# A hybrid attention and convolution block on one core: the second output projection takes its convolution features first, attention's splits are freed of later sums, nine background steps come sooner, and sixteen stores leave SP's queue for GpSimd's

## The chip, the cores and the metric

One core of a Trainium2 chip. The metric is the device time of one launch in microseconds. Before the change it is 2047.19 us, the median of three runs (2042.27 to 2048.67). The profiler's own execution of the same kernel took 2047.66 us, of which the span, first instruction to last, is 2045.9 us.

## The reference

One decoder layer over x of 2048 positions by 1024 features, all float32, with two mixers that read the same projection:

```python
h = rmsnorm(x, norm1_g)
q, k, v, g, a, c_b, c_c, c_h = split(h @ w_in)
o = gla_chunked(q, k, v, log_sigmoid(a @ w_gate_up + b_gate) / 16)   # 4 heads, a state carried along
o_gla = rmsnorm(o, gla_norm_g) * silu(g)                             # 512 features
o_conv = c_b * causal_depthwise_conv(c_c * c_h, conv_w)              # 512 features
x = x + concatenate([o_gla, o_conv]) @ w_out                         # the output projection
h2 = rmsnorm(x, norm2_g)
x = x + (silu(h2 @ w_gate) * (h2 @ w_up)) @ w_down
return rmsnorm(x, norm_f_g)
```

The linear attention (GLA) can be cut into chunks along the positions; a chunk needs the state that the chunk before it left. The convolution's features of a position do not depend on that state.

## The kernel before, in words

Positions lie in two halves of 1024, each of two blocks of 512. Features lie on the 128 partitions, and a product is built of 128x512 matmuls. Each float32 operand is split into a high and a low part, and three matmuls (high by high, high by low, low by high) make one product. Most of the large products are further made of seven block products in place of eight; their matmuls are L496, L497 and L498 in `product_step`.

The program runs: input projection of half 0, then of half 1; the output projection of half 0 (`first_out_proj`, L1335); that of half 1 (`out_proj`, L1411); and the feed-forward part of both halves. Between the matmuls of these, other work runs in the background. The generator `gla_half` takes the attention of one half in eight chunks of 128 positions. Each chunk fetches its data (`gla_fetch`), scales it (L1161 to L1164), makes scores (L1174, and a masked copy on VectorE at L1177), transposes (L1180, L1183), makes outputs (L1199, L1206) and the state (L1214, L1224, L1225), normalises (L1234 to L1240), and ends in `gla_finish`: transposes `ot` (L1249), the gate (L1250), a split into high and low part (L199), and two stores, of `g` and `osb`, into `s_gla` in HBM (in the profile sgla; each store takes one block and chunk).

`tick()` is called at set places of the main products and takes one background step at every second call. A generator that is wrapped in `hastened(steps, n)` (it stands in the kernel, and nothing calls it before the change) gets a step at every call whose count leaves 3 by 4 as well, until n of its steps are done. The final order on each engine is made by the tile scheduler from a model of the times; `behind(marks)` keeps an instruction behind those in `marks`. `gla_finish` puts its split behind `last_out + last_plus`, the newest sum of the main product at the time the program is written down.

`first_out_proj` takes the weights in four steps of d0 = 0, 2, 4, 6 (two output blocks of 128 features each). In each it makes seven products of the convolution features (four ticks), then 48 matmuls of the heads (L1386, L1392). `plus` (L1355) adds each result onto the residual `y` on VectorE; the finished `y` is stored as x1 (L1400; sx in the profile), and its squares are summed (`sum_squares`, L1269 to L1273).

`out_proj` has no seven products: for each of eight blocks k of 128 features it takes 12 matmuls in each d0 (L1421, L1422, L1424). Blocks 0 to 3 are the heads, from sgla, and 4 to 7 the convolution features, from sm. `build_mix` issues the sixteen loads (`op`, 512 KB each) in the order of k. During it the background normalises the x1 of half 0 for the feed-forward part (`h2_first`: `column_rstd` with the matmuls L218, the loads `h<-sx`, and L939 on VectorE).

Loads and stores all go through `load` (L152) and `store` (L155) on SP's queue, which issues them in order. Each waits for what it needs, and all that stands behind it on SP waits too; a DMA of SP also waits for the one that was issued eight before it. GpSimd (POOL) issues no DMA before the change.

Of the kernel before, what the change touches and what calls it, by code (L numbers as in the profile page):

```python
# [25 lines left out]
KD = D // P  # L26
# [4 lines left out]
GROUPS = (0, 2, 5, 8)  # L31
LAST_GROUP = GROUPS[-1]
EARLY = 7
EPS = 1e-6


# [17 lines left out]
def tile_hymba_block(ctx, tc, x, xt, win, wa, wgu, wout, wffn, wdown, wdown_first, small, out):  # L54
# [1022 lines left out]
    def in_proj(half, ops, raw=None, between=(), rest=None):  # L1077
        def units():
            if half == 0:
                yield unit(win[2], ops, raw=raw, between=between, rest=rest)  # L1080
            for u in range(0 if half else 3, 12):
                yield unit(win[u], ops, after=2 if half and u < 3 else None)

        units = units()
        for dst, i0 in ((s_kq, 0), (s_kq, 2), (s_v, 0), (s_v, 2)):
            if half == 0 and dst is s_kq:
                continue
            for r, j, c, p in next(units):
                store(dst[2 * half + j][i0 + r][:], settled(c, p)[:])
        for i0 in (0, 2):  # L1090
            for r, j, c, p in next(units):
                store(s_g[2 * half + j][i0 + r][:], silu(c, p)[:])
        if half:
            background.append(gla_half(half))
        for i0 in (0, 2):
            cc = {(r, j): settled(c, p) for r, j, c, p in next(units)}
            ch = {(r, j): c for r, j, c, _ in next(units)}
            for r in range(2):
                i = i0 + r
                left = halo[:, i, :]  # L1100
                for j in range(2):
                    s = tp.tile([P, PB + 2], F32, name="u", tag="t")
                    dve.tensor_tensor(s[:, 2:], ch[r, j][:], cc[r, j][:], ALU.mult)
                    act.activation(s[:, 0:2], left, AF.Copy)
                    left = s[:, PB : PB + 2]
                    y = cc[r, j]
                    act.activation(y[:], s[:, 0:PB], AF.Copy, scale=col(C_CW + i))
                    for n in (1, 2):
                        dve.scalar_tensor_tensor(
                            y[:], s[:, n : n + PB], col(C_CW + 4 * n + i), y[:], ALU.mult, ALU.add  # L1110
                        )
                if half == 0:
                    act.activation(halo[:, i, :], left, AF.Copy)
            for r, j, c, _ in next(units):
                y = cc[r, j]
                dve.tensor_tensor(y[:], c[:], y[:], ALU.mult)
                dst = s_mix[2 * half + j][i0 + r]
                if half:
                    pair_out(y, dst)
                else:  # L1120
                    store(dst[:], y[:])
# [136 lines left out]
    def plain_weights(src, n):  # L1258

        raw = rawp.tile([P, 4, PB], F32, name="raw", tag="raw")  # L1260
        load(raw[:, 0:n, :], src)
        for i in range(n):
            h = weight_quarter(raw[:, i, :])
            for k in range(4):
                yield h[:, 0, k * P : (k + 1) * P], h[:, 1, k * P : (k + 1) * P]
# [69 lines left out]
    def first_out_proj(y, conv, heads):  # L1335

        ssq = [
            tiny.tile([P, PB], F32, name=f"ssx{j}", tag=f"ssx{j}", bufs=1) for j in range(2)
        ]
        for d0 in range(0, KD, 2):  # L1340
            raw = raw_weights(wout[d0 // 2]).rearrange("p a (b e c) -> p (a b) e c", e=2, c=P)
            quads = [raw[:, k : k + 2, e, :] for e, k in ((0, 4), (0, 6), (1, 6), (1, 4))]
            w = unit_weights(None, quads)
            wh = [weight_quarter(raw[:, 0:HEADS, e, :]) for e in range(2)]

            def mul(i, o=None):
                first = o is None
                o = bank() if first else o
                n, m = PRODUCTS[i]
                for k in range(2):  # L1350
                    product_step(o, w[n], conv[m], k, first)
                return o

            def plus(at, o):
                last_plus[:] = [dve.tensor_tensor(y[at][:], o[:], y[at][:], ALU.add)]  # L1355
                last_out[:] = last_plus
                all_plus.extend(last_plus)

            oa = mul(0)
            plus((0, 0), oa)  # L1360
            ob = mul(1)
            plus((1, 1), ob)
            due("T3")
            tick()
            mul(2, oa)
            plus((0, 1), oa)
            due("B22")
            o = mul(3)
            tick()
            mul(4, oa)  # L1370
            plus((1, 1), oa)
            due("T4")
            mul(5, ob)
            plus((0, 1), ob)
            tick()
            mul(6, oa)
            plus((1, 0), oa)
            tick()
            following = residual(d0 + 2) if d0 + 2 < KD else None
            for e in range(2):  # L1380
                po = [bank() if e or j else o for j in range(2)]
                for k in range(HEADS):
                    c = slice(k * P, (k + 1) * P)
                    for j in range(2):
                        for part in range(2):
                            pe.matmul(  # L1386
                                po[j][:], wh[e][:, 0, c], heads[k][j][:, part, :],
                                start=k + part == 0 and e + j > 0, stop=False,
                                skip_group_check=True,
                            )  # L1390
                    for j in range(2):
                        pe.matmul(  # L1392
                            po[j][:], wh[e][:, 1, c], heads[k][j][:, 0, :], start=False,
                            stop=k == HEADS - 1, skip_group_check=True,
                        )
                    if k % 2:
                        tick()
                for j in range(2):
                    plus((e, j), po[j])
                    store(s_x1[j][d0 + e][:], y[e, j][:])  # L1400
                    sum_squares(ssq[j], y[e, j][:], d0 + e == 0)
            y = following
        return ssq

    def build_mix():
        def pair(b, k):
            return load_pair(s_gla[b][:, k] if k < HEADS else s_mix[b][k - HEADS])

        return [[pair(2 + j, k) for j in range(2)] for k in range(KD)]

    def out_proj(ops, ahead, rest):  # L1411
        ssq, half = [], 1
        ws = chain.from_iterable(plain_weights(wout[u], 4) for u in range(4))
        for d0 in range(0, KD, 2):
            o = {(e, j): bank() for e in range(2) for j in range(2)}
            for k in range(KD):
                for e in range(2):
                    wh, wl = next(ws)
                    for j in range(2):
                        m = ops[k][j]  # L1420
                        pe.matmul(o[e, j][:], wh, m[:, 0, :], start=k == 0, stop=False)  # L1421
                        pe.matmul(o[e, j][:], wh, m[:, 1, :], start=False, stop=False)  # L1422
                    for j in range(2):
                        pe.matmul(  # L1424
                            o[e, j][:], wl, ops[k][j][:, 0, :], start=False, stop=k == KD - 1
                        )
                if k == 3:
                    ys = {}
                    for e in range(2):
                        for j in range(2):  # L1430
                            ys[e, j] = tt("y")
                            load(ys[e, j][:], xt[2 * half + j, :, d0 + e, :])
                for _ in range(1 if d0 == KD - 2 else 2):
                    next(rest if d0 == KD - 2 else ahead, None)
                tick()
            if d0 == 0:
                ssq += [
                    tiny.tile([P, PB], F32, name=f"ssx{j}", tag=f"ssx{j}", bufs=1)
                    for j in range(2)
                ]  # L1440
            for e in range(2):
                for j in range(2):
                    b, dt = 2 * half + j, d0 + e
                    y = ys[e, j]
                    dve.tensor_tensor(y[:], y[:], o[e, j][:], ALU.add)
                    store(s_x1[b][dt][:], y[:])
                    sum_squares(ssq[j], y[:], dt == 0)
        return ssq
# [506 lines left out]
```

## Time and profile before

| | before |
|---|---|
| three runs, median (lowest to highest) | 2047.19 us (2042.27 to 2048.67) |
| profiled execution: time / span | 2047.66 / 2045.9 us |
| PE / PEld / DVE / ACT / POOL busy | 99 / 81 / 76 / 48 / 1 % of the span |
| mean granted clock of TensorE | 0.995 |
| second output projection begins on PE | 665.57 us |

The page gives busy shares for each engine and groups of instructions by source line. The views used here beside it are the list of waits of one engine (who it waited for, microseconds in total, how many times, the longest), the timeline (start, duration, instruction, and in square brackets the idle time ahead of it with what ended it), and tables of windows (a stretch in microseconds from the start of the span, its length, busy time of PE, PEld, DVE, ACT and POOL with their instructions, the granted clock as a share, the share of the DMA engines that was busy, GB/s). Matmuls overlap in the pipeline: one of 128x512 has a row of 0.39 us, but the next begins 0.23 us after it.

### The profile page before, as it was taken

What the parts mean: (1) busy time and instruction counts of PE and PEld (TensorE: products, weight loads), DVE (VectorE), ACT (ScalarE), POOL (GpSimd) and SP (SyncE); (2) the same over time, 40 slices, a digit from 0 to 9 for tenths busy, and PEclk for the clock granted to TensorE, in tenths of its full rate; (3) what the DMA queues carried; (4) which work ended last, traced back from release to release, by engine and by line L of the source; (5) the groups of instructions that cost most, each with busy time, mean ns of one, the idle gap of its engine ahead of it and who ended that gap; (6) DMA issues with size and microseconds to landing.
All of it is one profiled execution on the core that took longest, in us unless ns stands there. A gap on an engine that the chain in (4) does not pass through costs nothing.

```text
span 2045.9 us, 27026 instructions
## 1 busy us (share of the span) xinstructions
PE 2021.6 (99%) x9275; PEld 1658.7 (81%) x9275; DVE 1563.3 (76%) x2837; ACT 973.5 (48%) x1941; POOL 10.3 (1%) x17
## 2 busy tenths in 40 slices
PE   9999999999999999999999999999999999999998
PEld 8788878787877788888888888887888888888886
DVE  7888877668867597778777688887777777778886
ACT  6664455755534244444444453334444444454345
POOL 0000000000000000000000000000000000000001
PEclk9999999999999999999999999999999999999999
DMA  7356886644684893445445576577454444486653
GB/s 262 122 201 220 283 302 190 196 134 157 229 296 160 323 326 140 170 169 207 171 168 195 184 294 240 189 279 294 150 180 170 153 151 170 166 334 226 247 216 129
DMA packets 194634, 429.35 MB, mean 210 GB/s; under 512 B 20448, under 2 KB 67776, under 8 KB 185024
## 3 DMA queue, kind: packets, MB, share of 16 engines
q1 hardware_dynamic: 193776, 426.97, 58.9%
q8 instruction: 73, 1.20, 0.2%
q10 hardware_dynamic: 720, 0.66, 0.1%
q14 instruction: 65, 0.53, 0.1%
HBM read 279.69 MB, written 147.85 MB: 209 GB/s over the span
## 4 chain that ended last, share of the span: by engine, by line
PE 89%; DMA 5%; DVE 3%; ACT 2%; issue 1%; SPq 1%; POOL 0%; POOLq 0%; DVEq 0%; ACTq 0%
PE mm L496 26%; PE mm L498 26%; PE mm L497 26%; PE mm L1421 1%; PE mm L1424 1%; PE mm L1422 1%; DMA raw<-in_win_dram 1%; DMA op<-shT 1%; PE a_ps L1020 1%; PE mm L801 1%; PE mm L803 1%; PE mm L802 1%; PE mm L1741 1%; PE mm L1386 1%; PE o_ps L1199 1%
## 5 line engine op out<-in xcount | busy, mean ns | idle before, releaser
L496 PE MATMUL mm<-op,wq 128*128 128x512 f32 x2499 | 974.3, 393 | 4.1 <-ACT wq L198 1.5
L497 PE MATMUL mm<-op,wq 128*128 128x512 f32 x2499 | 972.3, 390 | 0.6 <-DVE op L199 0.5
L498 PE MATMUL mm<-op,wq 128*128 128x512 f32 x2499 | 962.1, 390 | 0.3
L198 ACT ACTIVATE wq<-raw 128x512 fp32r<-128x512 f32 (+2 forms) x628 | 361.8, 581 | 599.5 <-PE mm L498 477.6
L496 PEld LDWEIGHTS mm<-op,wq 128*128 128x128 f32 x2499 | 469.5, 188 | 107.6 <-ACT wq L198 4.6
L498 PEld LDWEIGHTS mm<-op,wq 128*128 128x128 f32 x2499 | 469.5, 188 | 99.9 <-DVE wq L199 1.9
L497 PEld LDWEIGHTS mm<-op,wq 128*128 128x128 f32 x2499 | 469.8, 188 | 98.6 <-DVE op L199 2.6
L199 DVE TENSOR_TENSOR wq<-raw,wq 128x512 fp32r<-128x512 f32 (+2 forms) x628 | 389.8, 625 | 165.2 <-ACT wq L198 163.6
L530 DVE TENSOR_TENSOR c<-mm,c 128x512 f32<-128x512 f32 x196 | 134.6, 687 | 71.8 <-PE mm L498 67.1
L530 DVE TENSOR_TENSOR y<-mm,y 128x512 f32<-128x512 f32 x185 | 126.5, 687 | 54.1 <-PE mm L498 53.8
L542 ACT ACTIVATE c<-mm 128x512 f32<-128x512 f32 x198 | 115.5, 589 | 33.1 <-PE mm L498 30.6
L448 DVE TENSOR_TENSOR raw<-raw 128x512 f32<-128x512 f32 (+2 forms) x190 | 116.5, 619 | 2.1
L198 ACT ACTIVATE wq<-s 128x512 fp32r<-128x512 f32 (+2 forms) x100 | 58.0, 580 | 101.3 <-PE mm L498 91.5
L448 DVE TENSOR_TENSOR s<-raw 128x512 f32<-128x512 f32 (+2 forms) x95 | 58.9, 620 | 33.9 <-DMA raw<-in_wffn_dram 17.8
L199 DVE TENSOR_TENSOR op<-op 128x512 fp32r<-128x512 f32 x100 | 66.3, 683 | 3.7 <-ACT op L198 3.5
L199 DVE TENSOR_TENSOR wq<-s,wq 128x512 fp32r<-128x512 f32 (+2 forms) x100 | 62.4, 624 | 2.2 <-ACT wq L198 1.4
L198 ACT ACTIVATE op<-op 128x512 fp32r<-128x512 f32 x100 | 59.2, 622 | 9.1 <-DMA op<-siT 3.2
L448 DVE TENSOR_TENSOR raw<-s,raw 128x512 f32<-128x512 f32 (+2 forms) x95 | 59.0, 621 | 1.3
L597 ACT ACTIVATE sg<-mm 128x512 f32<-128x512 f32 x26 | 15.5, 597 | 85.1 <-PE mm L498 85.1
L597 ACT ACTIVATE c<-c 128x512 f32<-128x512 f32 x78 | 48.9, 629 | 13.3 <-DVE c L530 10.6
L1421 PE MATMUL mm<-op,wq 128*128 128x512 f32 x128 | 50.8, 399 | 4.5 <-DMA op<-sgla 4.5
L1422 PE MATMUL mm<-op,wq 128*128 128x512 f32 x128 | 50.5, 395 | 0.0
(240 smaller groups left out, 1689.2 us busy)
## 6 DMA issues: line engine op xcount, KB each, us to landing
raw<-in_wffn_dram SPq DMA_DIRECT2D x44, 1024.0 KB, 5.9
sa_B<-so SPq DMA_DIRECT2D x47, 512.0 KB, 3.7
op<-sa_B SPq DMA_DIRECT2D x47, 512.0 KB, 6.9
raw<-in_win_dram SPq DMA_DIRECT2D x22, 1024.0 KB, 6.0
sa_T<-so SPq DMA_DIRECT2D x44, 512.0 KB, 4.4
op<-sa_T SPq DMA_DIRECT2D x44, 512.0 KB, 6.7
raw<-in_wdown_dram SPq DMA_DIRECT2D x24, 768.0 KB, 5.5
sx<-y SPq DMA_DIRECT2D x48, 256.0 KB, 4.1
```

The lines of the kernel that those rows point to most:

```text
L198: last_hi[:] = [act.activation(hi, src, AF.Copy)]
L199: last_lo[:] = [dve.tensor_tensor(lo, src, hi.bitcast(F32), ALU.subtract)]
L448: dve.tensor_tensor(*args)
L496: pe.matmul(o[:], wh, xh, start=first and k == 0, stop=False, skip_group_check=True)
L497: pe.matmul(o[:], wh, xl, start=False, stop=False, skip_group_check=True)
L498: return pe.matmul(o[:], wl, xh, start=False, stop=k == n - 1, skip_group_check=True)
L530: last_plus[:] = [dve.tensor_tensor(t[:], o[:], t[:], ALU.add)]
L542: last_out[:] = [act.activation(t[:], o[:], AF.Copy)]
L597: last_silu[:] = [act.activation(s[:], c[:], AF.Silu)]
L801: pe.matmul(acc[:], wq[:, 0, c], p[:, 0, :], start=first, stop=False)
L1421: pe.matmul(o[e, j][:], wh, m[:, 0, :], start=k == 0, stop=False)
L1422: pe.matmul(o[e, j][:], wh, m[:, 1, :], start=False, stop=False)
```

## The change

There are four edits. Line numbers are those of before; after the change they stand one to two higher.

1. **Features.** `LATE_HEADS` orders the blocks of `out_proj` as 4, 5, 6, 7, 0, 1, 2, 3. `build_mix` loads in that order, the matmuls follow it, `plain_weights` takes its quarters of the weights as 2, 3, 0, 1, and the marks for first and last go by the place in the order.
2. **Pace.** The attention of half 1 goes into the background as `hastened(gla_half(1), 9)`.
3. **Splits.** In `first_out_proj` only the sums of d0 = 0 are noted in `last_plus` and `last_out`; those of later d0 are not, so `gla_finish`'s split is no longer put behind them.
4. **Stores.** The sixteen stores of x1 in `first_out_proj` are issued by `pool.dma_start`.

```diff
+LATE_HEADS = 4, 5, 6, 7, 0, 1, 2, 3
...
-            background.append(gla_half(half))
+            background.append(hastened(gla_half(half), 9))
...
-        for i in range(n):
+        for i in (n // 2 + i if i < n // 2 else i - n // 2 for i in range(n)):
             h = weight_quarter(raw[:, i, :])
...
-                last_plus[:] = [dve.tensor_tensor(y[at][:], o[:], y[at][:], ALU.add)]
-                last_out[:] = last_plus
-                all_plus.extend(last_plus)
+                summed = dve.tensor_tensor(y[at][:], o[:], y[at][:], ALU.add)
+                all_plus.append(summed)
+                if d0 == 0:
+                    last_plus[:] = last_out[:] = [summed]
...
-                    store(s_x1[j][d0 + e][:], y[e, j][:])
+                    pool.dma_start(s_x1[j][d0 + e][:], y[e, j][:])
...
-        return [[pair(2 + j, k) for j in range(2)] for k in range(KD)]
+        return {k: [pair(2 + j, k) for j in range(2)] for k in LATE_HEADS}
...
-            for k in range(KD):
+            for n, k in enumerate(LATE_HEADS):
...
-                        pe.matmul(o[e, j][:], wh, m[:, 0, :], start=k == 0, stop=False)
+                        pe.matmul(o[e, j][:], wh, m[:, 0, :], start=n == 0, stop=False)
...
-                            o[e, j][:], wl, ops[k][j][:, 0, :], start=False, stop=k == KD - 1
+                            o[e, j][:], wl, ops[k][j][:, 0, :], start=False, stop=n == KD - 1
...
-                if k == 3:
+                if n == 3:
```

The instructions are the same in number and kind on PE, VectorE and ScalarE, and stand in another order only between the middle of the second input projection and the start of the feed-forward part. SP loses 16 DMAs, and POOL gains them.

The first place is SP's queue at the end of `first_out_proj`. Rows show the line, the destination and source with their buffer numbers, and the shape: `sgla3` is the attention's output of the last block of 512 positions, `op` an operand of `out_proj`, `sx` an x1 tile, `y` its source. Before the change:

```order
L155 DMA sx0_6_175<-y_6536 128x512
L155 DMA sx1_6_183<-y_6540 128x512
L155 DMA sgla3_234<-gt_6448 512x1x128
L155 DMA sgla3_234<-osb_6730 512x1x128
L152 DMA op_6837<-sgla3_234 128x1024
L152 DMA op_6839<-sgla2_233 128x1024
L152 DMA op_6841<-sgla3_234 128x1024
```

The same place after the change:

```order
L156 DMA sgla3_234<-gt_6308 512x1x128
L156 DMA sgla3_234<-osb_6590 512x1x128
L153 DMA op_6847<-sm2_3_212 128x1024
L153 DMA op_6849<-sm3_3_216 128x1024
L153 DMA op_6851<-sgla2_233 128x1024
L153 DMA op_6853<-sgla3_234 128x1024
L153 DMA op_6855<-sgla2_233 128x1024
L153 DMA op_6857<-sgla3_234 128x1024
```

The stores of x1 are gone from between, and two loads of convolution features stand ahead of those of the heads.

The second place is SP's queue at the start of `first_out_proj`, where `raw` is a block of w_out and `kq` belongs to a chunk of the attention. Before the change:

```order
L155 DMA sgla2_233<-gt_5313 512x1x128
L152 DMA y_5760<-in_xt_dram 128x512
L152 DMA y_5968<-in_xt_dram 128x512
L152 DMA raw_6384<-in_wout_dram 128x2048
L152 DMA y_5970<-in_xt_dram 128x512
```

After the change:

```order
L153 DMA op_6835<-sm2_0_209 128x1024
L153 DMA op_6837<-sm3_0_213 128x1024
L153 DMA op_6839<-sm2_1_210 128x1024
L153 DMA op_6841<-sm3_1_214 128x1024
L153 DMA y_5850<-in_xt_dram 128x512
L153 DMA y_6058<-in_xt_dram 128x512
L153 DMA op_6843<-sm2_2_211 128x1024
L153 DMA y_6060<-in_xt_dram 128x512
L153 DMA raw_6474<-in_wout_dram 128x2048
```

Five of the eight loads of sm for `out_proj` stand here now, ahead of the weights of the next d0.

The third place is PE at the passage into `out_proj`. `tot` is the sum for `column_rstd`; op_6835 is before the change the first head's operand, and after it that of the first convolution block. Before:

```order
L1392 MATMUL mm_6800<-op_5800,wq_6669 128x512
L1386 MATMUL mm_6799<-op_5802,wq_6669 128x512 x2
L1386 MATMUL mm_6800<-op_5804,wq_6669 128x512 x2
L1392 MATMUL mm_6799<-op_5802,wq_6669 128x512
L1392 MATMUL mm_6800<-op_5804,wq_6669 128x512
L1421 MATMUL mm_6867<-op_6835,wq_6873 128x512
L1422 MATMUL mm_6867<-op_6835,wq_6873 128x512
L1424 MATMUL mm_6867<-op_6835,wq_6873 128x512
L1421 MATMUL mm_6868<-op_6837,wq_6873 128x512
```

After the change, where the heads begin inside `out_proj`:

```order
L1426 MATMUL mm_6869<-op_6847,wq_6900 128x512
L1426 MATMUL mm_6870<-op_6849,wq_6900 128x512
L219 MATMUL tot_6936<-ssx0_5896,ones_92 128x512
L219 MATMUL tot_6947<-ssx1_5897,ones_92 128x512
L1423 MATMUL mm_6867<-op_6851,wq_6957 128x512
L1424 MATMUL mm_6867<-op_6851,wq_6957 128x512
L1423 MATMUL mm_6868<-op_6853,wq_6957 128x512
```

The first operand from sgla (op_6851) is now needed 48 matmuls of `out_proj` after its start, where before it is needed by the first one. The last transposes `ot` of the attention (L1249; after the change L1250) stand 30 matmuls ahead of the first one of `out_proj` before the change, and 114 ahead of it after the change.

## The prediction

> **What bounds the kernel now.** I read the page first, then the list of PE's waits, then tables of windows for the granted clock, then the timelines of PE, SP and VectorE around each wait. Two lines of the page and five of the list of waits:
>
> ```profile
> span 2045.9 us, 27026 instructions
> PE 2021.6 (99%) x9275; PEld 1658.7 (81%) x9275; DVE 1563.3 (76%) x2837; ACT 973.5 (48%) x1941; POOL 10.3 (1%) x17
> ```
>
> ```profile
> PE mm L1421 <- DMA op<-sgla: 4.5, 1, 4.5
> PE o_ps L1199 <- ACT c L542: 2.1, 1, 2.1
> PE v_ps L1183 <- issue: 1.4, 1, 1.4
> PE mm L1386 <- DMA op<-sgla: 0.4, 1, 0.4
> PE mm L496 <- DVE osb L1240: 0.3, 1, 0.3
> ```
>
> The kernel is bound by PE: 2021.6 of 2045.9 us are busy, and the change takes no matmul away. It can only gain where PE stands idle, or where an idle spell has slowed PE's clock. These five waits are all that PE has in the stretch that is reordered. The windows tell what a wait costs beyond its own length:
>
> ```profile
> 488.00:495.00 7.00, 6.82 (x19) 5.48 (x20) 4.72 (x10) 1.62 (x5) 0.00 (x0) 0.52 0.40 152
> 600.00:620.00 20.00, 18.28 (x97) 14.10 (x96) 14.29 (x37) 10.59 (x33) 0.00 (x0) 1.00 0.78 259
> 668.00:671.00 3.00, 0.05 (x1) 0.05 (x1) 0.64 (x2) 0.00 (x0) 0.00 (x0) 0.63 0.88 235
> 671.00:676.00 5.00, 5.00 (x11) 3.61 (x12) 0.00 (x0) 0.00 (x0) 0.00 (x0) 0.54 1.00 382
> ```
>
> After the waits of 2.1 and 4.5 us the granted clock falls to about half for some 7 us, though PE is busy again. Across the waits of 1.4 and 0.3 us (600 to 620) it stays at 1.00. So somewhere between 1.7 and 2.1 us of idleness a second price begins. After the wait at 486 us PE loses 7.00 x 0.48 = 3.4 us by the clock. After the one at 666 us much of the slow time falls into the idleness itself, and what is lost is 5.00 x 0.46 = 2.3 us.
>
> [...]
>
> **The long wait at the start of the second output projection.** PE, then SP, then VectorE:
>
> ```profile
> 658.41 0.49 PE L1249 MATMUL ot<-ident,osb 128*128 128x128 f32 x3
> ...
> 665.57 0.39 PE L1421 MATMUL mm<-op,wq 128*128 128x512 f32 x1
> 665.80 0.39 PE L1422 MATMUL mm<-op,wq 128*128 128x512 f32 x1
> 666.03 0.39 PE L1424 MATMUL mm<-op,wq 128*128 128x512 f32 x1
> 670.95 0.80 PE L1421 MATMUL mm<-op,wq 128*128 128x512 f32 x1 [4.54 <-DMA op<-sgla]
> ```
>
> ```profile
> 663.24 0.52 SPq L155 DMA_DIRECT2D sgla<-osb  x1
> 665.85 1.28 SPq L152 DMA_DIRECT2D op<-sgla  x3
> 667.22 1.16 SPq L155 DMA_DIRECT2D sx<-y  x2
> 668.43 2.86 SPq L152 DMA_DIRECT2D op<-sgla  x4
> 672.47 8.45 SPq L152 DMA_DIRECT2D op<-sm  x8
> 682.82 4.17 SPq L152 DMA_DIRECT2D y<-in_xt_dram  x4
> 687.94 4.16 SPq L152 DMA_DIRECT2D h<-sx  x4
> ```
>
> ```profile
> 662.53 0.68 DVE L199 TENSOR_TENSOR osb<-osb,gt 128x512 fp32r<-128x512 f32 x1
> ```
>
> The chain is serial: the last chunk's transposes at 658.41, its split at 662.53, its store at 663.24, the load that waits for the store at 665.85, and the matmul at 670.95, 12.5 us in all. PE has only 30 matmuls (7.2 us) to cover it. After the change 114 matmuls stand between these transposes and the first L1421, and the first 48 of the projection need sm alone. Matmuls follow each other by 0.23 us (665.57, 665.80, 666.03), so the chain gets 162 x 0.23 = 37 us in place of 7.2. Even with two loads of sm ahead of those of sgla on SP (8.45 us for eight, so 2.1) the margin is above 20 us. **This wait goes: 4.54 + 2.3 = 6.8 us.** What is late next there? The convolution operands: five of their eight loads stand about 90 us before their use, a sixth follows soon, and the last two stand ahead of the heads' loads.
>
> **The wait at 614 us.** PE, VectorE, SP:
>
> ```profile
> 615.39 0.63 PE L1183 MATMUL v_ps<-ident,vt 128*128 128x128 f32 x4 [1.39 <-issue]
> 616.36 0.47 PE L496 MATMUL mm<-op,wq 128*128 128x512 f32 x1 [0.33 <-DVE osb L1240]
> ```
>
> ```profile
> 590.18 0.42 DVE L448 TENSOR_TENSOR s<-raw 128x256 f32<-128x256 f32 x1
> ...
> 612.88 0.42 DVE L448 TENSOR_TENSOR s<-raw 128x256 f32<-128x256 f32 x1 [4.26 <-DMA raw<-in_wout_dram]
> ...
> 616.46 0.68 DVE L1355 TENSOR_TENSOR y<-mm,y 128x512 f32<-128x512 f32 x1
> ...
> 661.92 0.69 DVE L1355 TENSOR_TENSOR y<-mm,y 128x512 f32<-128x512 f32 x1 [0.76 <-PE mm L498]
> ```
>
> ```profile
> 576.78 0.33 SPq L152 DMA_DIRECT2D raw<-in_wout_dram  x1
> ...
> 597.46 1.21 SPq L155 DMA_DIRECT2D sx<-y  x1
> ...
> 604.51 0.36 SPq L152 DMA_DIRECT2D raw<-in_wout_dram  x1
> ```
>
> VectorE stood 4.26 us on a block of w_out that SP had issued only at 604.51; the attention's state (L1224) and norm (L1240) queued behind it, and PE waited 1.39 + 0.33 = 1.7 us for banks and operands. In the changed order that L448 stands behind L1224 and L1240 of the chunk, and x1 stores no longer stand ahead of the block on SP. **I count the 1.7 us as gained**, with nothing as the other end, since a late block then holds later sums instead. The 0.4 us of L1386 I leave where it is.
>
> **The wait at 486 us stays.** It comes from VectorE, which has no idle time ahead of it:
>
> ```profile
> 485.63 0.40 PE L497 MATMUL mm<-op,wq 128*128 128x512 f32 x1
> 488.18 1.19 PE L1199 MATMUL o_ps<-vt,scores 128*128 128x128 f32 x4 [2.15 <-ACT c L542]
> ```
>
> ```profile
> 470.00:488.00 18.00, 15.95 (x76) 12.27 (x74) 18.00 (x40) 10.32 (x25) 0.00 (x0) 1.00 0.72 239
> ```
>
> VectorE is busy for 18.00 of 18 us, and the order of VectorE up to that point is unchanged; the two matmuls ahead of L1199 move behind it. That shifts at most 0.1 us between idleness and slow clock, so 2.15 + 3.4 us remain.
>
> **The added costs.** The nine sooner steps bring no instruction; the first three chunks after 488 us come some 12, 22 and 26 us earlier, by the matmuls ahead of them at 0.23 us each. Their VectorE and ScalarE work moves into this stretch:
>
> ```profile
> 540.00:560.00 20.00, 20.00 (x106) 15.78 (x107) 18.23 (x42) 13.51 (x36) 0.00 (x0) 1.00 0.97 364
> 560.00:600.00 40.00, 39.44 (x213) 30.71 (x212) 29.68 (x70) 14.39 (x46) 0.00 (x0) 1.00 0.89 295
> ```
>
> VectorE has 1.8 us left in 540 to 560 and 10.3 in 560 to 600; half a chunk more in the former is about 3 us, which spills by about 1 us into the latter. I take nothing; the cover is the freedom behind 560, and if it is gone the price is the second case.
>
> The five early loads of sm are 2.6 MB in 560 to 600, where the DMA engines already are busy 0.89 of the time at 295 GB/s. At that rate they need 8.9 us, and 0.11 x 40 = 4.4 are free; so up to 4.5 us of lateness. I take nothing, because the block asked for at 576.78 was used at 590.18, and the one that is held up by the most traffic, asked for at 604.51, was ready at 612.88, 8.4 us after: 5 us of freedom for the former, about the same 4.5. The other end is the third case.
>
> The sixteen stores on POOL have no row before. Two DMA rows of the page bound them:
>
> ```profile
> sx<-y SPq DMA_DIRECT2D x48, 256.0 KB, 4.1
> y<-in_xt_dram SPq DMA_DIRECT2D x32, 256.0 KB, 5.7
> ```
>
> Who waits for a store is the next load of the same buffer. The tightest is the sum at 616.46, whose buffer serves the sum at 661.92: 45 us, of which store and load take 4.1 + 5.7. A store could come 35 us late and hold nobody. In the other direction, SP is free of sixteen issues, of which a long one is 1.21 us (597.46); that speeds loads that nobody but the wait at 614 us waits for. So nothing, both ways.
>
> [...]
>
> In the projection itself `column_rstd` moves behind 48 matmuls, 11 us after the start; it stood at 674.96, 9.4 us after it, because of the wait. The h loads at 687.94 stood behind fifteen operand loads, six of which are now gone from there, so the work of the feed-forward's operands is not later. Nothing.
>
> **The sum.** 2047.66 - 6.8 - 1.7 = 2039.1 us on the profiled execution, which is 0.5 us above the median of the runs. I predict 2039.
>
> **The rivals.**
>
> 1. *Forecast*, 0.56: 2036 to 2041. The lower end takes the 0.4 us as well and as much of smaller waits; the upper has the wait at 614 only shifted.
> 2. *A new short wait*, 0.20. The denser chunks before 600 us make PE stand once as at 486 us. For it speaks VectorE at 18.23 of 20; against it, of PE's waits between 500 and 600 us none is for VectorE now. 2.1 + 3.4 = 5.5 us: 2044.6.
> 3. *Late weights, slower than before*, 0.18. The five sm loads push the next block of w_out back by the 4.5 us worked out above. VectorE then stands 4.26 + 4.5 = 8.8 us where it stood 4.26. Of 4.26 us PE felt 1.7, so 2.5 are slack, and it would feel 6.2 and then half clock, 3.4: 2039.1 + 9.6 = 2048.7. With both later blocks late it is 2058. It decides from a lateness of about 3.5 us on, where loss and gain are equal. For it: 0.97 and 0.89 of DMA share. Against it: the 5 us of freedom that the first of these blocks has.
> 4. *Starved stores*, 0.03. If a store on POOL took over 35 us, SP would stand at the load behind it, and PE would wait once with half clock: 2044.6 or more.
> 5. *The heads still late*, 0.03. If sgla's loads are held by the operand buffers that the last products of `first_out_proj` use, the wait only moves 48 matmuls on: 2039.1 + 6.8 = 2045.9.
>
> **How the numbers follow.** What a measurement of this kernel can tell from no change is about 0.3%, 6.1 us: 2041.1 to 2053.3. The first case lies under it: faster 0.56. The second, fourth, fifth and the third with one block (0.08 of its 0.18) lie between: 0.34. The third with two lies above: 0.10. The range from 2036 to 2049 holds all but the last of these.
>
> **What would show it.** In the changed profile, L1421's wait on op<-sgla is gone from PE's list, and the windows between 640 and 700 us show a clock of 1.00; L1199 still waits about 2 us near 486 us, with one stretch of half clock behind it, the only one there. If there is a second stretch of half clock between 500 and 640 us, the forecast is wrong by 5 us or more; whether VectorE's wait ahead of it ends on raw<-in_wout (third case) or on nothing but its own work (second) tells which. POOL's stores that land much later than 4.1 us would speak for the fourth.

## The result, and the profile after

The changed kernel takes 2040.64 us, the median of seven runs (2037.56 to 2043.84), against 2046.37 us for the kernel before (2042.27 to 2048.67, seven runs). The ratio is 0.9971 with a 95% interval of 0.9959 to 0.9983: faster by 0.29%, just short of the 0.3% that I had taken as the least that can be told, though the interval lies clear of 1. The forecast was 2039.0 in a range of 2036 to 2049. The profiled execution took 2040.49 us with a span of 2038.3, 7.6 us below the span before.

The page's first lines, and PE's list of waits after the change, without the waits at the start and the end of the program:

```profile
span 2038.3 us, 27053 instructions
PE 2016.1 (99%) x9275; PEld 1656.9 (81%) x9275; DVE 1566.9 (77%) x2837; ACT 974.4 (48%) x1941; POOL 19.1 (1%) x33
```

```profile
PE mm L1388 <- DMA op<-sgla: 3.1, 1, 3.1
PE o_ps L1200 <- ACT c L543: 3.0, 1, 3.0
...
PE sc L1175 <- DVE kq L1165: 0.5, 1, 0.5
PE mm L497 <- DVE c L531: 0.5, 1, 0.5
```

L1421's wait on sgla (4.5 us) is gone, and so are those of L1183 (1.4) and L1240 (0.3). The wait at 486 us is still there, at 3.0 us and not 2.1. And one that was 0.4 us has become 3.1: L1388, the first projection's heads, on their loads. L1175 has a new wait of 0.5 us. The windows show what the two long ones cost beyond their length, and that the stretch around the second projection is whole:

```profile
488.00:495.00 7.00, 6.47 (x26) 5.25 (x27) 5.07 (x11) 2.48 (x6) 0.00 (x0) 0.76 0.49 184
575.00:580.00 5.00, 5.00 (x19) 3.95 (x20) 0.00 (x0) 0.60 (x1) 0.00 (x0) 0.66 1.02 405
640.00:660.00 20.00, 20.00 (x90) 16.55 (x89) 13.17 (x24) 6.34 (x11) 1.38 (x3) 1.00 0.80 298
660.00:680.00 20.00, 20.00 (x87) 15.84 (x86) 9.43 (x15) 6.69 (x12) 1.86 (x4) 1.00 0.77 304
```

The third last column is the granted clock. Behind the wait at 486 us it costs 7.00 x 0.24 = 1.7 us (3.4 before), and behind the new one 5.00 x 0.34 = 1.7. From 640 to 680 us PE is busy throughout at full clock; 660 to 680 holds 87 matmuls, where it held 56 before the change:

```profile
660.00:680.00 20.00, 15.46 (x56) 11.46 (x55) 9.09 (x15) 6.52 (x10) 0.00 (x0) 0.83 0.78 264
```

After the change, the last chunk's transposes, its store, the loads and the start of the projection, from the timelines of PE and SP:

```profile
639.23 0.60 PE L1250 MATMUL ot<-ident,osb 128*128 128x128 f32 x4
...
665.54 0.39 PE L1423 MATMUL mm<-op,wq 128*128 128x512 f32 x1
```

```profile
643.56 0.51 SPq L156 DMA_DIRECT2D sgla<-osb  x1
646.01 1.01 SPq L153 DMA_DIRECT2D op<-sm  x2
647.37 3.72 SPq L153 DMA_DIRECT2D op<-sgla  x6
652.16 0.33 SPq L153 DMA_DIRECT2D raw<-in_wout_dram  x1
652.59 2.02 SPq L153 DMA_DIRECT2D op<-sgla  x2
```

The heads' loads are all issued by 654.6, 11 us before the projection and some 22 before their first use. But the projection begins at 665.54, and before it began at 665.57: nothing that was gained ahead of it is left by then. The groups of the first matmul of a block (L1421 before, L1423 after) show that nearly the whole gain lies inside the projection:

```profile
L1421 PE MATMUL mm<-op,wq x128: 389/389/795, 665.6 to 760.5; 128*128 128x512 f32 x128
```

```profile
L1423 PE MATMUL mm<-op,wq x128: 389/389/791, 665.5 to 753.4; 128*128 128x512 f32 x128
```

From its first to its last: 94.9 us before, 87.9 after, 7.0 less, of a span that is 7.6 less.

### The profile page after: what moved, and what is told of

Read it like the earlier page. It is cut to its first block, busy times and chain, and to the rows that moved or that the text cites. A ratio compares the mean times of both kernels' runs of the same rounds, so it can differ in the third digit from the quotient of the medians.

```text
span 2038.3 us, 27053 instructions
## 1 busy us (share of the span) xinstructions
PE 2016.1 (99%) x9275; PEld 1656.9 (81%) x9275; DVE 1566.9 (77%) x2837; ACT 974.4 (48%) x1941; POOL 19.1 (1%) x33
## 4 chain that ended last, share of the span: by engine, by line
PE 91%; DMA 3%; DVE 3%; ACT 2%; issue 0%; SPq 0%; POOL 0%; POOLq 0%; DVEq 0%; ACTq 0%
PE mm L497 26%; PE mm L499 26%; PE mm L498 26%; PE mm L1426 1%; PE mm L1423 1%; PE mm L1424 1%; PE mm L1388 1%; DMA op<-shT 1%; PE a_ps L1021 1%; PE mm L802 1%; PE mm L804 1%; PE mm L803 1%; DMA op<-sgla 1%; PE mm L1743 1%; DMA raw<-in_win_dram 1%; PE o_ps L1200 1%
## 5 line engine op out<-in xcount | busy, mean ns | idle before, releaser
L497 PE MATMUL mm<-op,wq 128*128 128x512 f32 x2499 | 974.4, 393 | 2.5 <-ACT c L543 1.2
L497 PEld LDWEIGHTS mm<-op,wq 128*128 128x128 f32 x2499 | 469.5, 188 | 105.1 <-ACT wq L199 3.7
L1423 PE MATMUL mm<-op,wq 128*128 128x512 f32 x128 | 50.2, 392 | 0.0
```

What stands on the lines that cost most here:

```text
L497: pe.matmul(o[:], wh, xh, start=first and k == 0, stop=False, skip_group_check=True)
L1423: pe.matmul(o[e, j][:], wh, m[:, 0, :], start=n == 0, stop=False)
```

## The experiments

Each has its own runs of the kernel before on the same chip; ratios are to these. The first four take the change apart.

**Edit 1 alone.** Against the change:

```diff
-            background.append(hastened(gla_half(half), 9))
+            background.append(gla_half(half))
...
-                    pool.dma_start(s_x1[j][d0 + e][:], y[e, j][:])
+                    store(s_x1[j][d0 + e][:], y[e, j][:])
```

and the three lines of `plus` as before the change.

> Edit 1 alone: the convolution features come first in the second output projection, the other three edits are undone. The last transposes of the attention stand 33 rows-worth of matmuls ahead of the projection, as before the change, and the heads are needed 48 matmuls into it: 81 x 0.23 = 18.6 us for a chain that took 12.5. First theory (edits 1 and 2 each take the wait at the start of the projection away alone): 6.8 us faster than before, ratio 0.9967; the waits at 614 us (1.7) and at 486 us stay, and no wait of 3 us on the heads of half 0. Rival (both are needed, since two loads of 512 KB stand ahead of the heads'): a wait on sgla remains inside the projection, and the gain is under 3.5 us, ratio above 0.9983.

Measured: ratio 0.9973 (0.9962 to 0.9984), median 2041.75 against 2047.15. The wait on sgla in the second projection is gone. Three of its waits:

```profile
PE o_ps L1200 <- ACT c L543: 2.1, 1, 2.1
PE v_ps L1184 <- DMA vt<-sv: 1.6, 1, 1.6
PE mm L1387 <- DMA op<-sgla: 1.3, 1, 1.3
```

So one edit brings about the gain of all four (0.9971), within the noise. The first theory holds for the projection. It missed that the wait of the first projection's heads grows here too, from 0.4 to 1.3 us, without the sooner steps.

**Edit 2 alone.** The heads stay first, and `plus` and the stores are as before:

```diff
-LATE_HEADS = 4, 5, 6, 7, 0, 1, 2, 3
+LATE_HEADS = 0, 1, 2, 3, 4, 5, 6, 7
```

with `plain_weights` in the old order.

> Edit 2 alone: nine background steps come sooner, the heads stay first, splits and stores as before. The last transposes stand 119 matmuls ahead of the projection, 27 us. First theory: the wait at the start of the projection goes (6.8 us) and that at 614 us (1.7), but the new wait for the heads of half 0 near 572 us comes with its half clock (3.1 + 1.8 - 0.4 = 4.5): about 4 us faster than before, ratio 0.998. Rival (the new wait comes from the early loads of sm, edit 1): no wait near 572 us, 8.5 us faster, ratio 0.9958.

Measured: 0.9973 (0.9963 to 0.9982), 2042.84 against 2047.15: 4.3 us by the medians and 5.5 by the ratio, near the first theory's 4 us, but not by its sum. Three of its waits:

```profile
PE o_ps L1200 <- ACT c L543: 3.0, 1, 3.0
...
PE mm L1387 <- DMA op<-sgla: 1.7, 1, 1.7
PE v_ps L1184 <- issue: 1.7, 1, 1.7
```

The wait of the first projection's heads is 1.7 us and not 3.1, and the windows from 560 to 600 us show a clock of 1.00; the wait of v_ps, which I took to be gone, is there with 1.7. The wait in the second projection is gone by this edit alone too: from 660 to 680 us PE is busy for 20.00 us at a clock of 1.00. Each of the two edits takes the same 6.8 us, and the second to come finds nothing left.

**Without edit 2**, and **without edit 4**. One undoes the pace, the other puts the x1 stores back on SP; each is a line of the diff above.

> The change without edit 2 (edits 1, 3 and 4 are in). First theory: the wait at the start of the projection is gone, the new wait near 572 us is not there, that at 614 us stays or goes with the stores that have left SP: 6.8 to 8.5 us faster than before, ratio 0.9958 to 0.9967, at or below the whole change's. Rival (the new wait is not edit 2's): a wait of about 3 us near 570 us, and 3 us faster than before, ratio 0.9985.

> The change without edit 4: the sixteen x1 stores stay on SP. First theory (the stores' queue is worth nothing): as the whole change within 1 us, ratio to before 0.997, the same waits on PE. Rival (edit 4 carries part of the gain, because SP is free of sixteen issues ahead of the weights of w_out): the wait for raw near 614 us is back and 1.7 us or more are lost against the whole change, ratio 0.998 or above.

Measured: without the pace 0.9967 (0.9955 to 0.9980), 2041.28; without GpSimd's stores 0.9963 (0.9951 to 0.9976), 2040.62; both against 2047.15. Neither differs from the whole change. Without the pace the heads' wait near 570 us is 0.5 us, and the time is no better. Its profile has a wait of 2.2 us for ScalarE's split of an operand near 1396 us, which the change's profile doesn't have. That lies in the feed-forward part, where PE's order is the same in both, so one profile of each can't tell whether it belongs to the edit.

Without GpSimd's stores the heads' wait is 1.1 us, so PE's waits are not the same, as the first theory had them; and the rival is half right, as the weights of w_out are late again, though no time is lost. VectorE, and the wait of PE that follows:

```profile
617.72 0.43 DVE L449 TENSOR_TENSOR s<-raw 128x256 f32<-128x256 f32 x1 [2.35 <-DMA raw<-in_wout_dram]
```

```profile
PE v_ps L1184 <- DVE raw L449: 1.3, 1, 1.3
```

The timelines of PE in that kernel and in the changed one, at the heads' wait:

```profile
570.64 0.43 PE L1181 MATMUL kt_ps<-ident,kq 128*128 128x128 f32 x2
572.22 0.73 PE L1388 MATMUL mm<-op,wq 128*128 128x512 f32 x2 [1.14 <-DMA op<-sgla]
```

```profile
571.33 0.43 PE L1181 MATMUL kt_ps<-ident,kq 128*128 128x128 f32 x2
574.85 0.99 PE L1388 MATMUL mm<-op,wq 128*128 128x512 f32 x2 [3.09 <-DMA op<-sgla]
```

And SP in the same two kernels, ahead of the load that is waited for:

```profile
563.04 1.85 SPq L153 DMA_DIRECT2D gt<-sg  x4
...
566.95 0.39 SPq L153 DMA_DIRECT2D op<-sgla  x1
```

```profile
564.44 3.14 SPq L153 DMA_DIRECT2D gt<-sg  x4
...
569.11 0.40 SPq L153 DMA_DIRECT2D op<-sgla  x1
```

PE's order is the same in both, and the loads take 5.3 and 5.7 us to the matmul. The difference is when SP comes to the load: the four loads of `gt` ahead of it took SP 1.85 us in one and 3.14 in the other. The DMA engines were full up to 560 us in both (shares of 1.02 and 1.03 from 540 to 560), but not at these loads: from 562 to 568 us their share in the change is 0.19 to 0.48. Why SP took longer there is not shown. x1 stores play no part yet: GpSimd issues its first at 593.60. So with PE's order the same the wait varies; in the six kernels with that order, or with that order and the repeated transposes below, it is 1.1 to 3.1 us.

**Edit 3 undone**, with the three lines of `plus` as before the change.

> The change without edit 3: the attention's splits stay behind the sums of all four steps. PE's order is the same as with it. First theory: no difference beyond 1 us, ratio to before 0.997, PE's waits as in the whole change. Rival (the splits were late and held stores of sgla): a wait on sgla at the start of the heads in the second projection, and 2 us or more lost.

Measured: 0.9967 (0.9956 to 0.9979), 2039.83 against 2046.77, and waits as in the whole change (3.0 there is 2.9 here, 3.1 is 2.8). Edit 3 is worth nothing here.

Four further kernels try to take away the two waits that the change left.

**The attention later.** `pause(n)` gives n empty background steps, with n = 3 and n = 4:

```diff
+            background.append(pause(3))
             background.append(hastened(gla_half(half), 9))
```

> The change, and three empty background steps ahead of the attention of half 1, so that its first chunk comes later: 82 matmuls (19 us) now stand between that chunk's transposes (v_ps) and its outputs (o_ps), where none stood. First theory (the wait at 486 us costs its idleness and the half clock behind it): both go, 3.0 + 1.8 to 3.4 us, and the chain of the last chunk has 32 + 48 matmuls, 18 us for 12.5: 5 to 6 us faster than the whole change, ratio to before 0.9945. Rival (VectorE is the bound from 460 us on, so the wait is only put off to a later chunk): another wait of 2 us or more between 500 and 620 us with half clock, and the time of the whole change, ratio 0.997.

> As with three empty steps, but four: the first chunk's scores stand 84 matmuls later, its outputs 24 matmuls (5.5 us) behind its transposes, and the last transposes 26 matmuls ahead of the second projection, 74 ahead of the first need of the heads (17 us). First theory: the wait at 486 us is gone, VectorE having 5.5 us at a time when it is not full; no wait for sgla in the projection; ratio 0.9945. Rival (17 us are too few for the chain with two loads of sm ahead of it): a wait of 2 us or more on op<-sgla inside the projection, ratio 0.997 or above.

Measured: three steps 0.9992 (0.9983 to 1.0001), four 1.0016 (1.0007 to 1.0025). The rival of the first kernel has the mechanism right and the time too short (0.997); for the second kernel both theories miss. The wait of o_ps is gone from both lists, and others stand in its place. With four, in the list of waits:

```profile
PE mm L497 <- DVE y L1357: 5.9, 1, 5.9
PE mm L497 <- DVE kvs L1226: 2.6, 1, 2.6
PE mm L497 <- ACT c L543: 2.6, 2, 1.4
PE sc L1176 <- issue: 2.4, 1, 2.4
```

Later chunks meet the weights of the first projection on VectorE, and PE waits there for sums and for the attention's state. With four steps VectorE itself stands 9.7 us, in three waits, on blocks of w_out. The place of the attention's start is worth more than the one wait at it.

**Convolution stores on GpSimd too.**

```diff
-                    pair_out(y, dst)
+                    pair_out(y, dst, pool.dma_start)
```

where `pair_out` takes the issuing function as an argument.

> The change, and the stores of the convolution features of half 1 (sm) also on GpSimd's queue; they stood between the loads of half 0's heads on SP. First theory (those loads are late by their place in SP's queue): each is issued 1 to 3 us sooner, and the wait on op<-sgla near 572 us falls from 3.1 us to under 1.5 and brings no half clock: 2 to 4 us faster than the whole change, ratio 0.9955. Rival (that wait's length is the DMA engines' load at the time, 1.03 of 540 to 560, and differs from run to run): the same time as the whole change within 1 us, ratio 0.997.

Measured: 0.9987 (0.9978 to 0.9996), 2044.38 against 2046.77, so both theories miss: it loses some of the gain. The heads' wait falls only to 2.1 us, a new one of 2.6 (L497, on VectorE's hsq) stands behind it, and the windows from 580 to 600 show 0.91 of the clock. The scheduler also placed the attention's pieces in another order, so this run doesn't tell what the queue alone does.

**PE kept busy.** In `gla_scores` of the first chunk alone, the transposes into kt_ps are repeated once its copy has been taken; nothing reads them:

```diff
+        for i in range(8 if (b, t) == (2, 0) else 0):
+            pe.transpose(kt_ps[:, i % 2, :], kq[:, i % 2, :], ident[:])
```

This was put into the change with 8 and with 16 transposes, into edit 1 alone with 8, and into the change without edit 4 with 16.

> The change, and eight transposes (about 1 us) that repeat the first chunk's kt_ps after it has been copied, while PE waits near 486 us; their result is not read. All else on PE stands in the same order. First theory (the drop of the clock follows a spell without any work on PE of some 2 us): the wait of 2.96 us is cut into pieces under 2, the clock between 488 and 495 stays at 1.00, and 1.7 to 3.4 us go: ratio to before about 0.996. Rival (the drop comes with any light load of that stretch): the clock still falls behind 488 us, ratio 0.997.

> As with eight, but sixteen repeated transposes, about 2 us. First theory: no idle piece over 1 us is left there, the clock stays at 1.00, and o_ps starts no later than before (VectorE and ScalarE set that), so 1.7 to 3.4 us go: ratio about 0.996, as with eight or better. Rival: the transposes come too late, push o_ps back by up to 1 us and save nothing: ratio 0.9975.

> Edit 1 alone, and the eight repeated transposes near 486 us. First theory: edit 1 alone takes the wait at the start of the second projection away (6.8 us, in the profile of edit 1 alone), the wait of 2.15 us at 486 us is cut and with it its half clock (1.7 to 3.4 us), and no new wait with half clock comes near 572 us: the fastest of all, 8 to 9 us faster than before, ratio 0.9958. Rival (the waits at 570 to 615 us, 1.3 to 1.6 us each, are as dear as the whole change's): ratio 0.997.

> Edits 1, 2 and 3 with the sixteen repeated transposes, and the x1 stores on SP as before the change. First theory (edit 4 is worth nothing, the repeated transposes save the half clock near 486 us): clock 1.00 between 488 and 495 us, the time of the kernel with sixteen transposes and GpSimd's stores within 1 us, ratio 0.996. Rival (GpSimd's stores carry a gain once the half clock is gone): ratio above 0.997.

| | ratio (95%) | median, before |
|---|---|---|
| the change, 8 transposes | 0.9963 (0.9949 to 0.9977) | 2038.3, 2047.49 |
| the change, 16 transposes | 0.9961 (0.9948 to 0.9974) | 2037.58, 2047.49 |
| edit 1 alone, 8 | 0.9965 (0.9952 to 0.9977) | 2039.48, 2047.49 |
| edits 1, 2, 3, with 16 | 0.9955 (0.9941 to 0.9968) | 2037.93, 2047.54 |

The order of the rest of the program is the same but for a few matmuls next to this place. PE's timeline with 8, and then the window behind it:

```profile
485.41 1.09 PE L1188 MATMUL kt_ps<-ident,kq 128*128 128x128 f32 x8 [0.96 <-ACT ee L1185]
487.41 0.68 PE L1202 MATMUL o_ps<-vt,scores 128*128 128x128 f32 x4 [0.90 <-ACT c L543]
```

```profile
488.00:495.00 7.00, 7.00 (x40) 5.65 (x40) 5.39 (x13) 3.27 (x12) 0.00 (x0) 1.00 0.33 124
```

Counted from the transposes into v_ps the attention's outputs start no sooner (3.6 us after them, 3.5 in the change), but the idle time is cut into 0.96 and 0.90 us, and the clock stays at 1.00: 40 matmuls in these 7 us, where the change had 26. It does so in all four, while all eight profiles without such transposes or empty steps have a lowered clock there (0.83 to 0.91 from 480 to 500 us). So at this place the lowered clock goes with the idle spell of 2.1 to 3.0 us: nothing else was taken away. All four medians lie 1 to 3 us under the change's; the intervals overlap with its own, so that they beat it is likely and not shown, while each beats the kernel before. Edit 1 alone with 8 was expected to be the fastest of all and has the highest median of the four; its profile has a wait of 1.9 us near 612 us, of v_ps on its load.

## Why the prediction was right, and where it was not

**What bounds the kernel**: right. PE is busy for 99% in both, and the whole difference is in its waits and their clock.

**The long wait, 6.8 us**: right, in place and size. The projection is 7.0 us shorter from its first to its last matmul, and it is edit 1 that does it, or edit 2; either is enough. I had added the room that both give (114 and 48 matmuls) without asking what each gives alone.

**The wait at 614 us, 1.7 us counted as gained, with nothing against it**: this is the step that failed. It is gone from the changed profile, but the projection starts at the same moment as before. What took its place was the wait of 0.4 us at L1386, of which I wrote that I leave it where it is: it became 3.1 us and 1.7 us of lowered clock. I looked for new waits at VectorE and at the weights, and costed the denser chunks there. I didn't follow what they do to the loads of the *first* projection's heads: those stand on SP behind the fourteen small loads of a chunk, and in PE's order one v_ps and one pair of heads fewer stand ahead of the use that waits. In the profiles without the sooner steps this wait is 0.4 to 1.3 us, in the eight with them and without empty steps 1.1 to 3.1. The second rival had such a wait at nearly the right price (2.1 + 3.4 there, 3.1 + 1.7 here) from other parts; its cause was not VectorE but a DMA.

**The wait at 486 us, unchanged at 2.15 + 3.4**: right in that it stays, and wrong in its parts, of which I let at most 0.1 us move; it measured 3.0 + 1.7.

These do not add up to the equal start: 1.7 us are gained at 614 us and 0.9 at 486 (5.5 before, 4.7 after), and 4.4 are lost at 572 (3.1 + 1.7 - 0.4) and 0.5 at the new wait of L1175, so the projection should start about 2.3 us later. It doesn't. By the starts of PE's rows from 480 us to the projection, the waits and the lowered clock taken off, the same matmuls took about 2.5 us less after the change (an estimate), some 1.1 of it in the attention's outputs (L1199 and L1206). Why they did stays open. That the time lies in the first case all the same is in part luck: a loss that the sum hadn't was made up by gains that it hadn't either.

**Late weights**: did not happen in the change. No wait on raw is in PE's list, with a DMA share of 1.03 from 540 to 560 us and 1.05 from 580 to 600. Nor did the early loads of sm make the heads late: SP issues them from 579.88 us on, behind the load that PE waits for at 572.

**GpSimd's stores, nothing**: right. They took 5.4 us to land in the median (2.5 to 7.7), against 4.1 for such stores before, and nobody waited; with them on SP the time is the same. But the stores do bear on the wait at 614 us. In the six profiles with them on SP VectorE waits for that block of w_out (0.3 to 4.8 us); in the six with them on GpSimd, the two with empty steps left aside, it does not. So part of that wait's end is edit 4's, and no time shows it. Where the 1.3 us more come from is not shown; without the pace the median is 4.3.

**The signs**: L1421's wait is gone and the clock from 640 to 700 us is 1.00, as I had said. But there is a second stretch of half clock between 500 and 640 us, from 575 us on, by which I had called the forecast wrong by 5 us or more. It was off by 1.6. So the profile shows the second rival's new short wait, and the time is that of the first case.

**The range and the chances**: 2040.64 lies in the first case's 2036 to 2041. By the median it is a gain of 0.28%, so on the border between the two chances that I had set at 0.56 and 0.34.

## What to carry to other kernels

Two edits against the same wait are worth one: before adding their gains, ask what each leaves for the other. Where work is brought forward, follow each load that it passes on its queue to its first use, above all the loads whose wait is already above zero; a wait of 0.4 us marks a place without slack. And where a lowered clock follows a wait of PE, cheap matmuls that nobody reads are worth trying: here the second price of waits of 2.1 to 3.1 us was 1.7 or 3.4 us, about as large as the spell.

## What the runs showed of the hardware

The price of an idle spell isn't fixed. The same wait of 2.96 us cost 7.00 x 0.24 = 1.7 us by the clock in the change and 7.00 x 0.45 = 3.2 in edit 2 alone:

```profile
488.00:495.00 7.00, 6.55 (x19) 5.22 (x20) 4.99 (x10) 1.89 (x5) 0.00 (x0) 0.55 0.47 178
```

From 480 to 500 us the mean clock is 0.91 in the change and 0.83 in edit 2 alone, so 20.00 x 0.17 = 3.4 us in the latter, of which 0.2 fall ahead of 488 us. The wait's length doesn't tell which of the two it will be. With 2.1 us the clock of these 20 us was 0.83 before the change, and 0.91 in edit 1 alone and without the pace. With 2.9 to 3.0 us it was 0.91 in the change and without GpSimd's stores, and 0.83 in edit 2 alone, with edit 3 undone and with the convolution stores on GpSimd.

Finer windows show where the clock is lowered. In the traces of before and of the change it is 1.00 or 0.50 and nothing between, and the end of the program aside each has two stretches at 0.50. Before the change both last 6.83 us, in the change both 3.41, so they cost 3.4 and 1.7 us where PE is busy throughout. Before:

```profile
487.85:494.67 6.82, 6.49 (x18) 5.20 (x19) 4.87 (x10) 1.77 (x5) 0.00 (x0) 0.50 0.43 163
668.75:675.58 6.83, 4.63 (x10) 3.47 (x11) 0.00 (x0) 0.00 (x0) 0.00 (x0) 0.50 0.98 332
```

The change, each stretch with the 3.41 us ahead of it:

```profile
486.41:489.82 3.41, 1.29 (x9) 1.08 (x9) 3.41 (x9) 2.56 (x6) 0.00 (x0) 1.00 0.95 343
489.82:493.23 3.41, 3.41 (x9) 2.74 (x9) 2.71 (x7) 1.00 (x3) 0.00 (x0) 0.50 0.40 151
571.74:575.15 3.41, 0.32 (x2) 0.30 (x2) 1.69 (x7) 0.78 (x2) 0.00 (x0) 1.00 0.87 256
575.15:578.57 3.42, 3.42 (x12) 2.68 (x11) 0.00 (x0) 0.60 (x1) 0.00 (x0) 0.50 1.01 404
```

Nor is there one length of a spell from which a drop falls due, as I had put it between 1.7 and 2.1 us. With four empty steps a spell of 2.59 us ahead of 555.08 left the clock at 1.00:

```profile
555.08 0.47 PE L497 MATMUL mm<-op,wq 128*128 128x512 f32 x1 [2.59 <-DVE kvs L1226]
```

```profile
552.00:556.00 4.00, 1.41 (x9) 1.07 (x8) 2.44 (x6) 3.83 (x14) 0.00 (x0) 1.00 0.89 254
556.00:560.00 4.00, 4.00 (x20) 3.27 (x19) 4.00 (x13) 1.57 (x4) 0.00 (x0) 1.00 1.04 384
```

Of two waits of 1.9 us near 570 us, one with 8 transposes came with a clock of 0.91 from 560 to 580 us; the other, with 16 and the stores on SP, left it at 1.00. What decides whether a spell of 2 to 3 us lowers the clock, and for how long, these runs don't settle.

Nor do they show what makes the runs of one kernel differ by some 6 us (2037.56 to 2043.84 in the change). One sign that waits come and go beside the edits lies in the feed-forward part, where PE's order is the same in all these kernels: near 1400 us edit 2 alone, without the pace and without GpSimd's stores each have a wait of 1.4 to 2.2 us for ScalarE's split, and the change and edit 1 alone have none.
